# One-hot operands of the dense expert gates, built token by token instead of four tokens at a time

## The chip, the cores and the metric

The kernel runs on one core of a Trainium2 chip. The metric is the device time of one execution in microseconds (us). For the kernel before it is 4725.49 us, the median of 3 runs (4711.8 to 4730.83).

## What is computed

The reference is a two-layer trunk over 256 context and 512 latent tokens of width 1024. Each layer is a mixer followed by a PEER feed-forward: for every token, 8 heads select 16 of 16384 experts each, that is 128 pairs (e1, e2) with expert = 128·e1 + e2, and a softmax gate for each. The output is

```
act = gelu(sum_d pu[expert] * t) * gate
out = sum over the 128 chosen experts of act * pv[expert]
```

The change touches one step of this. For the tokens that are computed densely (all 16384 experts at once), the kernel needs a matrix G with G[e2, e1] = the sum of the gates of a token's chosen pairs (e1, e2), zero elsewhere, 128 x 128 numbers a token.

## The kernel before

Four of the latent token tiles (128 tokens each) of layer 0 and three of layer 1 are dense; the other tiles gather the rows of their experts from memory with an indirect DMA on POOL and add them up on DVE.

The function `peer` first routes (scores, top 16 by key half), then has a stage with two kinds of work in it. The first kind: `select` (lines 1034 to 1084) and `dense_gates` (lines 1086 to 1118) for each tile. The second: `up_part` (line 1228), which multiplies the tokens with one block of 128 experts of `pu` in 24 matmuls of f32r numbers (line 393), splits the weights into a high part on ACT (line 380) and a low part on DVE (line 383, tile `wlo`), and applies the gelu on ACT. 60 blocks of layer 0 and 48 of layer 1 are done there. Steps of the gather (lines 1127, 1132, 1141) are attached to them by `pace` and `gstep`. The next stage multiplies the gelu outputs with the gates, which it reads back from memory (tile `gt`, line 1290, all tiles of a block at once), so it starts when the last gates of the last tile have been written.

In `dense_gates` the 128 pairs of a token lie on the 128 partitions: e1, e2 and the gates are transposed (line 1095) and copied by ACT to SBUF (line 1096), the gates as a float16 high part and, on DVE (line 1097), a low part. Then, for every 4 tokens (`GW = 4`), DVE makes two tiles:

- `o`, two one-hot matrices (of e1 and of e2) for 4 tokens, by comparing a table of the numbers 0 to 127 (`iob`, line 248) with e1 and e2 (line 1105),
- `og`, the one-hot of e1 times the high and the low part of the gate (line 1107).

Both hold their numbers with the token as the innermost index, so that a token's 128 numbers lie 4 float16 numbers, or 8 bytes, apart. TensorE then makes G for each token in 2 matmuls of 128 columns (line 1113): the one-hot of e2 is the stationary operand, the two halves of `og` are the moving ones, and both add up in one piece of PSUM (`gps`). ACT copies it out in two pieces (line 1115) into `gbig`, and 64 tokens of it are written to memory with two DMAs of 2 MB (line 1118), issued from ACT's queue.

A dense tile has 32 such groups of 4 tokens: 128 groups in layer 0 and 96 in layer 1, 224 in all. `o` and `og` have 4 buffers each (`OB`), `gps` 3, `gbig` 3. The framework orders the instructions of each engine when the kernel is built, and each engine runs its queue in that order.

Of the kernel before, what the change touches and what calls it, by code (L numbers as in the profile page):

```python
# [8 lines left out]
F32 = mybir.dt.float32  # L9
F32R = mybir.dt.float32r  # L10
BF16 = mybir.dt.bfloat16
F16 = mybir.dt.float16
# [3 lines left out]
OP = mybir.AluOpType  # L16
# [16 lines left out]
GSC = 32768.0  # L33
GW = 4
# [34 lines left out]
OB = 4  # L69
# [126 lines left out]
class Net:  # L196
# [26 lines left out]
    def setup(self, st):  # L223
        tc, nc = self.tc, self.nc
        p = st.enter_context(tc.tile_pool(name="const", bufs=1))
        self.kt = p.tile(list(_CONST["consts"].shape), F32, name="kt")
        self.ct = p.tile([128, NCOLS], F32, name="ct")
        self.cc = p.tile([128, 8, 2], F32, name="cc")
        self.load(self.cc, self.I["cc"])
        self.load(self.kt, self.I["consts"])  # L230
        self.load(self.ct, self.I["cols"])
        self.eps = p.tile([128, 4], F32, name="eps")
        for j, v in enumerate((1e-6, 64e-5, 1e-5, 0.0)):
            nc.vector.memset(self.eps[:, j:j + 1], v)
        self.ones = p.tile([1, 2], F32, name="ones")
        nc.vector.memset(self.ones, 1.0)
        self.sc = p.tile([128, 8, 2], F32, name="sc")
        nc.scalar.activation(out=self.sc, in_=self.cc, func=AF.Silu)
        o = _COFF
        w = p.tile([128, 21], F32, name="shw")  # L240
        nc.vector.tensor_tensor(out=w, in0=self.cols("l0_shift_prev", 0, 21), in1=self.cols("l0_shift_next", 0, 21), op=OP.add)
        nc.vector.tensor_scalar(out=w, in0=w, scalar1=-1.0, scalar2=1.0, op0=OP.mult, op1=OP.add)
        self.shw = w
        ka = p.tile([128, 6], F32, name="ka1")
        nc.vector.tensor_scalar(out=ka, in0=self.cols("l0_k_a", 0, 6), scalar1=-1.0, scalar2=1.0, op0=OP.mult, op1=OP.add)
        self.ka1 = ka
        self.iob = p.tile([128, 128, GW], F16, name="iob")
        nc.vector.tensor_copy(self.iob, self.k("iota")[:, :, None].to_broadcast([128, 128, GW]))
        self.io16 = p.tile([128, 16, 16], BF16, name="io16")
        nc.vector.tensor_copy(self.io16, self.k("iota", 0, 16)[:, :, None].to_broadcast([128, 16, 16]))  # L250

        dp = st.enter_context(tc.tile_pool(name="modd", bufs=1, space=DR))
        self.odp = dp
        self.modd = [dp.tile([2, 6144], F32, name=f"modd{l}") for l in range(2)]
        self.modcol = [p.tile([128, 4, 8, 2], F32, name=f"modcol{l}") for l in range(2)]
# [830 lines left out]
    def dense_gates(self, e1, e2, gate, gd, sp, gp, pp, pt):  # L1086

        nc = self.nc
        V = nc.vector


        ee, gg = sp.tile([128, 2, 128], F16, name="gxe"), sp.tile([128, 2, 128], F16, name="gxg")
        for dst, x, sc in ((ee[:, 0], e1, 1.0), (ee[:, 1], e2, 1.0), (gg[:, 0], gate, GSC)):
            p = pt.tile([128, 128], F32, name="gtp")
            nc.tensor.transpose(p, x.rearrange("p a b -> p (a b)"), self.k("ident"))
            nc.scalar.mul(out=dst, in_=p, mul=sc)
        V.scalar_tensor_tensor(out=gg[:, 1], in0=p, scalar=GSC, in1=gg[:, 0], op0=OP.mult, op1=OP.subtract)
        W, H = GW, 64
        for h0 in range(0, 128, H):
            gh = [gp.tile([128, 64, H], F32, name="gbig") for _ in range(2)]  # L1100
            for t0 in range(h0, h0 + H, W):
                w = slice(t0, t0 + W)
                o = sp.tile([128, 2, 128, W], F16, name="o12", bufs=OB)
                og = sp.tile([128, 2, 128, W], F16, name="og", bufs=OB)
                V.tensor_tensor(out=o, in0=self.iob[:, None].to_broadcast([128, 2, 128, W]),
                                in1=ee[:, :, None, w].to_broadcast([128, 2, 128, W]), op=OP.is_equal)
                V.tensor_tensor(out=og, in0=o[:, 0:1].to_broadcast([128, 2, 128, W]),
                                in1=gg[:, :, None, w].to_broadcast([128, 2, 128, W]), op=OP.mult)
                for k0 in range(0, W, 4):
                    p = pp.tile([128, 4, 128], F32, name="gps")  # L1110
                    for j in range(4):
                        for i in range(2):
                            nc.tensor.matmul(p[:, j, :], o[:, 1, :, k0 + j], og[:, i, :, k0 + j], start=(i == 0), stop=(i == 1))  # L1113
                    for i, g in enumerate(gh):
                        nc.scalar.mul(out=g[:, :, t0 - h0 + k0:t0 - h0 + k0 + 4].rearrange("p e t -> p t e"), in_=p[:, :, i * 64:i * 64 + 64],  # L1115
                                      mul=1.0 / GSC)
            for i, g in enumerate(gh):
                nc.scalar.dma_start(gd[h0 // H, :, i * 64:i * 64 + 64, :], g)
# [501 lines left out]
```

## Time and profile before

| | before |
|---|---|
| median of 3 runs | 4725.49 us |
| the profiled execution | 4744.95 us |
| its span | 4743.2 us |
| mean granted TensorE clock | 0.944 |
| PE busy | 4296.7 us (91%) |
| DVE busy | 3613.7 us (76%) |
| ACT busy | 1705.7 us (36%) |
| POOL busy | 1687.5 us (36%) |

The span runs from the first to the last instruction of the profiled execution; some 2 us lie around it. Busy shares are means over stages with different limits. In the rows further down, L1113 is line 1113 of the kernel; PE is TensorE's matmul and PEld its weight load, which overlap; DVE is VectorE, ACT ScalarE, POOL GpSimd. A matmul's duration runs from its start to its modelled end, and consecutive matmuls overlap. "x128" counts instructions.

### The profile page before, as it was taken

To read this page: it belongs to the slowest core of one execution; us is meant where nothing else is said; L and a number is where in the kernel's file an instruction comes from. 1 tells how busy PE (TensorE), PEld (TensorE's weight loads), DVE (VectorE), ACT (ScalarE), POOL (GpSimd) and SP (SyncE) were. 2 spreads that over 40 slices of the span, in tenths; PEclk is the share of its full clock that TensorE was granted. 3 is DMA by queue.
4 is the path that set the end of the run, shared out by engine and by line. 5 is a ranking of instruction groups with operands and counts; after the bars stand their busy time and mean duration, and the time that the engine had idled before them with its cause. 6 is when DMAs were issued, how large, how long until landed. Compare 5 with 4: busy or idle time off the path is not lost.

```text
span 4743.2 us, 69779 instructions
## 1 busy us (share of the span) xinstructions
PE 4296.7 (91%) x26113; PEld 3547.1 (75%) x26113; DVE 3613.7 (76%) x6615; ACT 1705.7 (36%) x2825; POOL 1687.5 (36%) x1178
## 2 busy tenths in 40 slices
PE   7998899985869998999999999779999979999998
PEld 5775567874647887877777788666789968888887
DVE  2776566689889997877778787685499877788775
ACT  3443123332213555222222222346335543333333
POOL 2332112214644322444444443372321224444430
PEclk9998998987889998999999999889999979999999
DMA  4444773335778776888889888310235589999984
GB/s 165 100 107 105 267 258 116 113 121 167 229 245 284 251 261 244 309 309 302 299 311 308 302 302 281 117 35 25 86 111 189 211 318 331 329 336 338 333 289 152
DMA packets 487279, 1061.99 MB, mean 224 GB/s; under 512 B 95094, under 2 KB 265846, under 8 KB 477206
## 3 DMA queue, kind: packets, MB, share of 16 engines
q1 hardware_dynamic: 371740, 594.02, 38.2%
q0 software_dynamic: 110592, 402.70, 24.3%
q10 hardware_dynamic: 4608, 60.82, 3.1%
q8 instruction: 205, 3.36, 0.3%
q14 instruction: 134, 1.10, 0.1%
HBM read 927.83 MB, written 129.56 MB: 223 GB/s over the span
## 4 chain that ended last, share of the span: by engine, by line
PE 49%; DVE 15%; issue 14%; DMA 12%; POOL 8%; ACT 2%; SPq 0%; POOLq 0%; DVEq 0%; ACTq 0%
PE pS L393 14%; PE acc L1286 9%; POOL row L1127 7%; DMA row<-in_l_pv_dram,gi 6%; PE gps L1113 4%; PE sm L755 2%; DMA row<-in_l_pur_dram,gi 2%; PE pjl L393 2%; PE pq L393 2%; DVE row L1132 2%; PE aO L1567 1%; PE pjc L393 1%; PE sm L803 1%; PE acc L1315 1%; DVE rows L1141 1%
## 5 line engine op out<-in xcount | busy, mean ns | idle before, releaser
L1127 POOL DMA_INDIRECT row<-in_l_pv_dram,gi x384 | 541.6, 1411 | 874.4 <-DVE rows L1141 748.0
L393 PE MATMUL pS<-h2hi,wlo 128*128 128x512 f32 (+1 forms) x2048 | 753.9, 368 | 28.2 <-DVE wlo L383 28.2
L393 PE MATMUL pS<-h2hi,whi 128*128 128x512 f32 (+1 forms) x2048 | 755.1, 369 | 19.9 <-ACT a L1232 14.8
L393 PE MATMUL pS<-h2lo,whi 128*128 128x512 f32 (+1 forms) x2048 | 752.8, 368 | 0.0
L1127 POOL DMA_INDIRECT row<-in_l_pur_dram,gi x384 | 482.7, 1257 | 696.7 <-DVE ga L1132 519.9
L380 ACT CAST whi<-wraw 128x1024 fp32r<-128x1024 f32 x327 | 344.2, 1054 | 825.7 <-PE pS L393 644.3
L1132 DVE CUSTOM_DVE_ANT_0 row<-row,rows 128x1024 f32<-128x1024 f32 x384 | 486.7, 1272 | 196.6 <-DMA row<-in_l_pur_dram,gi 195.2
L1141 DVE SCALAR_TENSOR_TENSOR rows<-row,ga,rows 128x1024 f32<-128x1024 f32 x381 | 496.7, 1304 | 157.0 <-DMA row<-in_l_pv_dram,gi 154.8
L1286 PE MATMUL acc<-vhi,ahi 128*128 128x512 f32 x1536 | 470.1, 392 | 12.9 <-ACT ahi L380 12.8
L1286 PE MATMUL acc<-vlo,ahi 128*128 128x512 f32 x1536 | 479.3, 392 | 1.8 <-DVE vlo L383 1.7
L1286 PE MATMUL acc<-vhi,alo 128*128 128x512 f32 x1536 | 470.3, 391 | 0.4 <-DVE alo L383 0.4
L393 PEld LDWEIGHTS pS<-h2hi,wlo 128*128 128x128 f32 x2048 | 390.6, 191 | 72.9 <-DVE wlo L383 32.0
L393 PEld LDWEIGHTS pS<-h2hi,whi 128*128 128x128 f32 x2048 | 391.2, 191 | 66.8 <-ACT a L1232 15.7
L393 PEld LDWEIGHTS pS<-h2lo,whi 128*128 128x128 f32 x2048 | 391.0, 191 | 43.5
L383 DVE TENSOR_TENSOR wlo<-wraw,whi 128x1024 fp32r<-128x1024 f32 x266 | 342.0, 1286 | 58.6 <-ACT whi L380 58.0
L380 ACT CAST vhi<-vraw 128x1024 fp32r<-128x1024 f32 x256 | 265.2, 1051 | 232.8 <-DMA vraw<-in_l_pv_dram 113.1
L383 DVE TENSOR_TENSOR vlo<-vraw,vhi 128x1024 fp32r<-128x1024 f32 x256 | 309.7, 1220 | 43.8 <-ACT vhi L380 43.5
L1286 PEld LDWEIGHTS acc<-vhi,ahi 128*128 128x128 f32 x1536 | 287.7, 188 | 69.3 <-ACT ahi L380 15.1
L1286 PEld LDWEIGHTS acc<-vlo,ahi 128*128 128x128 f32 x1536 | 289.4, 189 | 64.8 <-DVE vlo L383 3.3
L1286 PEld LDWEIGHTS acc<-vhi,alo 128*128 128x128 f32 x1536 | 288.6, 188 | 62.9 <-DVE alo L383 2.2
L380 ACT CAST ahi<-a32f 128x384 fp32r<-128x384 f32 (+1 forms) x148 | 83.5, 564 | 613.1 <-DVE a32f L1302 312.6
L1115 ACT ACTIVATE gbig<-gps 128x256 f32<-128x256 f32 x448 | 235.5, 660 | 165.5 <-PE gps L1113 141.2
(459 smaller groups left out, 8306.8 us busy)
## 6 DMA issues: line engine op xcount, KB each, us to landing
wraw<-in_l_pu_dram SPq DMA_DIRECT2D x256, 512.0 KB
vraw<-in_l_pv_dram SPq DMA_DIRECT2D x256, 512.0 KB
gd<-gbig ACTq DMA_DIRECT2D x28, 2048.0 KB
mw<-in_l_mod_w_dram SPq DMA_DIRECT2D x48, 1024.0 KB
gt<-gd SPq DMA_DIRECT2D x64, 512.0 KB
wraw<-in_l_pq_dram SPq DMA_DIRECT2D x48, 512.0 KB
gt<-gd SPq DMA_DIRECT2D x64, 384.0 KB
ab<-arb SPq DMA_DIRECT2D x24, 768.0 KB
```

The source lines that it names most:

```text
L380: e.copy(out=hi, in_=src)
L383: return (e_lo or nc.vector).tensor_tensor(out=lo, in0=src, in1=hi.bitcast(F32), op=OP.subtract)
L393: nc.tensor.matmul(ps, a[:, k, :], b[:, k, t0:t0 + n], start=s, stop=e)
L755: self.nc.tensor.matmul(ps[q, i, :], fa(par, i), fb(par, i), start=True, stop=True)
L803: nc.tensor.matmul(ps[par][:, i, :], bk[PH[par], j], ar[PH[par], j], start=True, stop=True)
L1113: nc.tensor.matmul(p[:, j, :], o[:, 1, :, k0 + j], og[:, i, :, k0 + j], start=(i == 0), stop=(i == 1))
L1115: nc.scalar.mul(out=g[:, :, t0 - h0 + k0:t0 - h0 + k0 + 4].rearrange("p e t -> p t e"), in_=p[:, :, i * 64:i * 64 + 64], mul=1.0 / GSC)
L1127: nc.gpsimd.indirect_dma_start(out=r, out_offset=None, in_=self.I[f"l{l}_{src}"], in_offset=bass.IndirectOffsetOnAxis(ap=idx[:, s:s + 1], ...
L1132: V.tensor_tensor_reduce(out=r, in0=r, in1=acc, scale=1.0, scalar=0.0, op0=OP.mult, op1=OP.add, accum_out=act[:, s:s + 1])
L1141: V.scalar_tensor_tensor(out=acc, in0=r, scalar=act[:, s:s + 1], in1=acc, op0=OP.mult, op1=OP.add)
L1286: nc.tensor.matmul(acc[t][h2], x[:, q], y[:, h2 * 512:(h2 + 1) * 512], start=s, stop=z)
L1315: nc.tensor.matmul(p, x[:, 384:512], y[:, c], start=s, stop=z)
```

## The change

Each token's numbers now lie next to each other, and gate and one-hot are made in one operation. The table `iob` has one copy of 0 to 127 instead of four. The tile `o` holds the one-hot of e2 only. For each token DVE runs three TENSOR_SCALAR instructions over 128 float16 numbers: one compares the table with the token's e2 (one number for each partition, read from a column of `ee`), two compare it with e1 and multiply by the high or the low part of the gate (two numbers for each partition, from columns of `ee` and `gg`). Since those columns are read as scalars, `ee` and `gg` are float32 now; the gate's high part is first rounded to float16 (`g16`) and copied back, one more ACT instruction a tile. Matmuls, PSUM, the copies out and the DMAs stay as they are.

```diff
-        self.iob = p.tile([128, 128, GW], F16, name="iob")
-        nc.vector.tensor_copy(self.iob, self.k("iota")[:, :, None].to_broadcast([128, 128, GW]))
+        self.iob = p.tile([128, 128], F16, name="iob")
+        nc.vector.tensor_copy(self.iob, self.k("iota"))
...
-        ee, gg = sp.tile([128, 2, 128], F16, name="gxe"), sp.tile([128, 2, 128], F16, name="gxg")
-        for dst, x, sc in ((ee[:, 0], e1, 1.0), (ee[:, 1], e2, 1.0), (gg[:, 0], gate, GSC)):
+        ee, gg = sp.tile([128, 2, 128], F32, name="gxe"), sp.tile([128, 2, 128], F32, name="gxg")
+        for dst, x in ((ee[:, 0], e1), (ee[:, 1], e2), (None, gate)):
             p = pt.tile([128, 128], F32, name="gtp")
             nc.tensor.transpose(p, x.rearrange("p a b -> p (a b)"), self.k("ident"))
-            nc.scalar.mul(out=dst, in_=p, mul=sc)
+            if dst is not None:
+                nc.scalar.copy(out=dst, in_=p)
+        g16 = sp.tile([128, 128], F16, name="gx16")
+        nc.scalar.mul(out=g16, in_=p, mul=GSC)
+        nc.scalar.copy(out=gg[:, 0], in_=g16)
         V.scalar_tensor_tensor(out=gg[:, 1], in0=p, scalar=GSC, in1=gg[:, 0], op0=OP.mult, op1=OP.subtract)
...
-                w = slice(t0, t0 + W)
-                o = sp.tile([128, 2, 128, W], F16, name="o12", bufs=OB)
-                og = sp.tile([128, 2, 128, W], F16, name="og", bufs=OB)
-                V.tensor_tensor(out=o, in0=self.iob[:, None].to_broadcast([128, 2, 128, W]),
-                                in1=ee[:, :, None, w].to_broadcast([128, 2, 128, W]), op=OP.is_equal)
-                V.tensor_tensor(out=og, in0=o[:, 0:1].to_broadcast([128, 2, 128, W]),
-                                in1=gg[:, :, None, w].to_broadcast([128, 2, 128, W]), op=OP.mult)
+                o = sp.tile([128, W, 128], F16, name="o12", bufs=OB)
+                og = sp.tile([128, 2, W, 128], F16, name="og", bufs=OB)
+                for j in range(W):
+                    t = slice(t0 + j, t0 + j + 1)
+                    V.tensor_scalar(out=o[:, j], in0=self.iob, scalar1=ee[:, 1, t], scalar2=None, op0=OP.is_equal)
+                    for i in range(2):
+                        V.tensor_scalar(out=og[:, i, j], in0=self.iob, scalar1=ee[:, 0, t], scalar2=gg[:, i, t],
+                                        op0=OP.is_equal, op1=OP.mult)
...
-                            nc.tensor.matmul(p[:, j, :], o[:, 1, :, k0 + j], og[:, i, :, k0 + j], start=(i == 0), stop=(i == 1))
+                            nc.tensor.matmul(p[:, j, :], o[:, k0 + j], og[:, i, k0 + j], start=(i == 0), stop=(i == 1))
```

## Rows read from the trace of the kernel before

**Rows 1.** Busy us by stretch: stretch, length, PE, PEld, DVE, ACT, POOL, clock, DMA.

```profile
1480.00:1810.00 330.00, 330.00 (x1813) 276.88 (x1812) 311.15 (x542) 171.49 (x289) 111.58 (x66) 1.00 0.73 258
1810.00:1860.00 50.00, 37.67 (x283) 32.11 (x281) 40.60 (x67) 36.42 (x73) 0.00 (x0) 0.71 0.52 212
3560.00:3780.00 220.00, 218.16 (x1421) 210.83 (x1419) 196.33 (x373) 130.41 (x222) 46.60 (x15) 1.00 0.54 194
3780.00:3840.00 60.00, 38.47 (x262) 34.62 (x262) 52.19 (x84) 30.34 (x59) 14.54 (x12) 0.70 0.72 260
```

**Rows 2.** The chain that ended last, 1380 to 1960 us: start, us, what.

```profile
1474.39 14.97 PE pS L393 x66
1489.36 2.85 PE gps L1113 x24
...
1817.16 8.19 DMA gd<-gbig
...
1861.73 7.21 PE pS L393 x23
```

**Rows 3.** DVE's groups, 1480 to 1860 us: busy, mean ns, idle before.

```profile
L1105 DVE TENSOR_TENSOR o<-iob,gxe 128x1024 f16<-128x1024 f16 x128 | 89.0, 713 | 20.5 <-PE gps L1113 19.5 <-ACT gxe L1096 0.9
L1107 DVE TENSOR_TENSOR og<-o,gxg 128x1024 f16<-128x1024 f16 x128 | 84.7, 684 | 0.1
L383 DVE TENSOR_TENSOR wlo<-wraw,whi 128x1024 fp32r<-128x1024 f32 x46 | 63.1, 1372 | 4.3 <-ACT whi L380 4.0
L1141 DVE SCALAR_TENSOR_TENSOR rows<-row,ga,rows 128x1024 f32<-128x1024 f32 x33 | 50.6, 1533 | 0.0
...
L1066 DVE TENSOR_SCALAR tb<-taf 128x128 f32<-128x128 bf16 x3 | 0.7, 221 | 0.0
```

**Rows 4.** DVE's timeline behind the last up part of layer 0: start, us, what.

```profile
1829.71 0.69 DVE L1107 TENSOR_TENSOR og<-o,gxg 128x1024 f16<-128x1024 f16 x1
1830.32 0.69 DVE L1105 TENSOR_TENSOR o<-iob,gxe 128x1024 f16<-128x1024 f16 x1
```

**Rows 5.** Other DVE operations, whole span: by line (min/median/max ns) or by group.

```profile
L1081 DVE TENSOR_TENSOR tex<-teq,txf x8: 1205/1222/2310, 1096.3 to 1157.5; 128x1024 f32<-128x1024 bf16 x8
...
L1319 DVE TENSOR_TENSOR acc<-acc,acc 128x512 f32<-128x512 f32 x126 | 86.3, 685 | 9.2 <-PE acc L1315 9.2
...
L315 DVE TENSOR_SCALAR nx<-nx,ns 128x1024 f32<-128x1024 f32 x6 | 4.5, 754 | 0.2
L600 DVE TENSOR_SCALAR kds<-ag,ct,ka 128x768 f32<-128x768 f32 x6 | 4.0, 674 | 0.0
...
L336 DVE TENSOR_SCALAR nh<-pt,modcol x32: 396/410/413, 1143.6 to 3398.5; 128x128 f32<-128x128 f32 x32
```

**Rows 6.** DVE's timeline around two TENSOR_SCALARs in a row.

```profile
1143.62 0.72 DVE L336 TENSOR_SCALAR nh<-pt,modcol 128x128 f32<-128x128 f32 x2
1144.26 0.68 DVE L990 TENSOR_TENSOR ox<-ox,om 128x512 f32<-128x512 f32 x1
```

**Rows 7.** TensorE, whole span: line 1113 (min/median/max ns) and groups of line 393.

```profile
L1113 PEld LDWEIGHTS <-o x1792: 111/117/147, 1489.2 to 3843.6; 128*128 128x128 f16 x200
L1113 PE MATMUL gps<-og,o x1792: 273/297/330, 1489.2 to 3843.7; 128*128 128x128 f16 x200
...
L393 PE MATMUL pS<-h2lo,whi 128*128 128x512 f32 x1024 | 404.3, 395 | 0.0
L393 PE MATMUL pS<-h2lo,whi 128*128 128x384 f32 x1024 | 348.5, 340 | 0.0
...
L393 PEld LDWEIGHTS pS<-h2lo,whi 128*128 128x128 f32 x2048 | 391.0, 191 | 43.5
```

**Rows 8.** ACT's copy of the gates ahead of a tile's groups, by line.

```profile
L1096 ACT ACTIVATE gxg<-gtp x7: 270/278/320, 1474.5 to 3761.8; 128x128 f16<-128x128 f32 x7
```

**Rows 9.** The full stretches of rows 1, line 1113 alone: PE, PEld, clock, DMA.

```profile
1480.00:1810.00 330.00, 97.73 (x750) 81.03 (x751) 1.00 0.73 258
...
3560.00:3780.00 220.00, 69.94 (x536) 57.86 (x536) 1.00 0.54 194
```

## The prediction

> **What bounds the kernel now.** I began with the busy time by slice, where the two stages in which gates are made stand out by a full TensorE, and cut them into stretches [rows 1]. In layer 0 (1480 to 1810 us) PE is busy for all of 330 us, at full clock; but DVE is busy for 311.15 of them as well. Then comes a tail of 50 us in which only gates are left: the clock is down to 0.71 and no engine is full. Layer 1 has the same shape: 220 us with PE at 218.16 and DVE at 196.33, and a tail of 60 us. So two engines are nearly full, and what the change takes from the one and gives to the other decides.
>
> The chain of waits for that time [rows 2] goes through PE: up-part matmuls (66 in 14.97 us, 227 ns apart) in turn with gate matmuls (24 in 2.85 us, 119 ns apart), in the tail through gates and the 2 MB writes of them (8.19 us), and the first work of the next stage starts at 1861.73, behind the last gates. That stage's end is thus the end of the gates, wherever they are held up.
>
> In DVE's groups of the stage [rows 3] the two instructions of the gates take 89.0 and 84.7 us for 128 groups. They share the queue with the low parts of the weights (63.1 us), on which the up-part matmuls wait, with the steps of the gather (50.6 us at line 1141), by which POOL gets its row buffers back, and with the selection of the next tile. DVE runs its queue in order, so whatever is added to a group delays all of these.
>
> **The change part by part: DVE.** Removed are 2 TENSOR_TENSORs for 4 tokens. In a row they start 0.60 us apart, with a duration of 0.685 [rows 4]: 85 ns of each lie under its neighbour. A group costs 2 x 600 = 1200 ns.
>
> Added are 12 TENSOR_SCALARs of 128 numbers: 4 that read one column as their scalar and 8 that read two. The trace has no such instruction in float16, so I build its price from the nearest rows.
> - Rate. A TENSOR_TENSOR of f32 takes 685 ns for 512 numbers and 1222 for 1024, so 1.05 ns a number [rows 5]; the float16 one does 1024 in 685 [rows 4], twice as fast.
> - Fixed part. If TENSOR_SCALAR of f32 takes half of 1.05 ns a number, what is left is 221 - 67 = 154 ns with no column (line 1066) [rows 3], 754 - 537 = 217 with one (line 315), 674 - 403 = 271 with two (line 600) [rows 5]. Each column costs about 60 ns.
> - Does the column's part hide under the instruction before it? Two instructions of line 336, 410 ns each alone and with two columns [rows 5], take 0.72 us together, and the next starts 0.64 after the first [rows 6]: 320 each, 90 hidden, no more than with TENSOR_TENSOR. It doesn't hide.
> - Numbers. If float16 doubles the rate of TENSOR_SCALAR as it does that of TENSOR_TENSOR, 128 numbers take 33 ns; if not, 67. I take 33, because the doubling is what the nearest float16 row shows, and keep 67 for the range.
>
> So one column costs 33 + 217 - 87 = 163 ns, two cost 33 + 271 - 87 = 217, and a group 4 x 163 + 8 x 217 = 2388 ns, twice the 1200 of before. At 67 ns it is 2796. The lower bound is a column that costs nothing: 12 x (33 + 154 - 87) = 1200, no difference at all. [...]
>
> On DVE that adds 1188 ns x 128 = 152 us to layer 0 and x 96 = 114 us to layer 1, 266 in all. DVE's idle time in these stretches is 380 - 351.75 = 28 us and 280 - 248.52 = 31 us [rows 1]; part of it is the wait for buffers in the tails, which slower gates hide. I count half of it as used up: 266 - 30 = **236 us**, with 206 and 266 as the bounds.
>
> **TensorE.** All 1792 gate matmuls get contiguous operands. The weight load is short already, 117 ns against 191 for f32 [rows 7], so I expect nothing there. The matmul is not: f32r takes 395 ns for 512 columns and 340 for 384, 55 for 128 columns, which would make 230 for 128; float16 at a step of 8 bytes takes 297 [rows 7]. That 67 ns more, and the 119 ns from one matmul to the next [rows 2] where the f32r pace of 227 for 512 (213 of columns and 14) would give 67, say that the step costs some 52 ns a matmul. The gain lies between 0 and 52 x 1792 = 93 us of PE time. I count it at nothing for the span: with DVE full, PE waits for splits and one-hots, and a faster matmul makes that wait longer. What hides it is DVE's added 266 us; without that cover the gain is a rival below.
>
> **The rest.** One more ACT copy a tile at 278 ns [rows 8], with the low part of the gate waiting for it: at most 7 x 0.3 = 2 us if nothing covered it, but ACT is half idle [rows 1] and DVE has other tiles' work; I count 1. The smaller table is made once, at the start, and I count nothing for it. No DMA is added or moved. POOL's gathers wait longer for row buffers within the stage; their number there is fixed, and their end is not what the next stage waits for. ACT's copies out of PSUM come later, not more often.
>
> **Sum.** 4744.95 + 236 + 1 = 4982 us for the profiled execution. That execution stood 19.5 us above the median of the runs; against the median it is 4725.49 + 237 = **4962 us**, and the forecast's own range 4930 to 4995.
>
> **The rivals.**
> 1. *The columns are free, and TensorE was the bound (faster).* If the fetch of the columns runs under the instruction before, a group stays at 1200 ns. Then DVE is unchanged and PE's 52 ns count: in the full stretches the 750 gate matmuls of layer 0 [rows 9] give 39 us, cut off by DVE's idle 330 - 311 = 19, and the 536 of layer 1 give 28, cut off at 220 - 196 = 24 [rows 1]. That is -43 us, 4682. The point from which it decides is a group of some 1300 ns; line 336 speaks against it, since its two columns did cost in a row [rows 6]. Chance 0.13. [...]
> 2. *Columns are free and the layout does nothing for PE (no change).* The 119 ns would then come from something other than the step. Time 4725, chance 0.04. [...]
> 3. *No doubling.* 2796 - 1200 = 1596 ns x 224 = 358, less 30: 5053. Line 1066 with a 16-bit input and an f32 output doesn't tell. Chance 0.15.
> 4. *TensorE's clock.* With PE waiting, the clock may fall as in the tails (0.71 and 0.70 [rows 1]). [...] Chance 0.07.
> 5. *Columns half hidden.* A group of about 1800 ns: 134 less 30, 4830. Chance 0.05.
>
> **How the numbers follow.** The forecast has 0.56. A measurement of this kernel can tell about 0.5% (24 us) from no change. Faster by more is rival 1, 0.13; the same is rival 2, 0.04; the rest is slower, 0.83. The range from 4825 to 5085 holds the forecast and rivals 3 to 5, 0.83 together, with the upper bound of rival 3; likeliest alone, 4930 to 4995.
>
> **What would show it.** In the changed profile 2688 TENSOR_SCALARs stand in place of the 448 TENSOR_TENSORs, at about 250 ns (896) and 304 ns (1792); 284 and 338 if float16 doesn't double. Twelve in a row take 2.4 us. DVE is busy for over 95% of two stages that end some 140 and 95 us later, PE's idle time ahead of lines 393 and 1113 names DVE, and the clock there lies under 1.00. The gate matmuls take about 235 ns, some 67 apart where they run in a row. The forecast is wrong if twelve take under 1.5 us, or if the order of DVE's queue, which is made anew when the kernel is built, puts splits and gates so that PE finishes its up parts much later than the gates.

## The result, and the profile after

The changed kernel takes 5052.85 us (median of 4 runs, 5043.1 to 5054.38), the kernel before 4728.16 in the runs beside it: a ratio of 1.0681 with a 95% interval of 1.0659 to 1.0702, or some 325 us more by the medians. The forecast was 4962, its range 4825 to 5085.

The page of the kernel after, its busy times and three of its strips (40 slices of 126 us):

```profile
span 5041.3 us, 72050 instructions
PE 4440.3 (88%) x26113; PEld 3500.4 (69%) x26113; DVE 3886.5 (77%) x8855; ACT 1711.7 (34%) x2832; POOL 1649.6 (33%) x1178
PE   7997999967678679999999999779978779999998
DVE  2776576798999996677778888674699977787675
PEclk9997999978878658999999999899988579999999
```

DVE's busy time has grown from 3613.7 to 3886.5 us, by 273. In both stages with the gates (slices 12 to 15 and 31 to 32) its strip now reads 9, and there the strips of PE and of its clock have fallen.

DVE's and TensorE's groups of the gates (busy, mean ns of one, idle before). Lines 1111 and 1113 are the new one-hots and gates, 1119 the matmul that was 1113:

```profile
L1113 DVE TENSOR_SCALAR og<-iob,gxe,gxg 128x128 f16<-128x128 f16 x1792 | 524.2, 345 | 0.0
L1111 DVE TENSOR_SCALAR o<-iob,gxe 128x128 f16<-128x128 f16 x896 | 243.6, 279 | 2.0 <-ACT gxe L1097 2.0
...
L1119 PE MATMUL gps<-og,o 128*128 128x128 f16 x1792 | 380.7, 255 | 176.3 <-DVE og L1113 113.4 <-ACT gbig L1121 1.1 <-issue 0.2
```

DVE's timeline in layer 0's stage, two tokens in a row (start us, us, what):

```profile
1702.29 0.56 DVE L1113 TENSOR_SCALAR og<-iob,gxe,gxg 128x128 f16<-128x128 f16 x2
1702.74 0.28 DVE L1111 TENSOR_SCALAR o<-iob,gxe 128x128 f16<-128x128 f16 x1
1702.90 0.56 DVE L1113 TENSOR_SCALAR og<-iob,gxe,gxg 128x128 f16<-128x128 f16 x2
```

A token takes 1702.90 - 1702.29 = 0.61 us, a group of four some 2.43 us; before it was 1.20 [rows 4]. An instruction with one column starts 0.16 us before the next (1702.74 to 1702.90), one with two columns some 0.22 (half of 1702.29 to 1702.74). TensorE's idle time ahead of the gate matmuls names DVE for 113.4 of 176.3 us, as it had to.

Then the stages. Busy us by stretch (stretch, length, PE, PEld, DVE, ACT, POOL, clock, DMA) of the kernel after; layer 0 from its first gate to its last and from there to the next stage, then layer 1 the same way:

```profile
1473.00:1916.00 443.00, 332.86 (x1542) 179.40 (x1541) 441.76 (x1821) 176.77 (x322) 59.17 (x36) 0.67 0.36 135
1916.00:2061.00 145.00, 138.75 (x596) 113.77 (x597) 74.32 (x64) 42.20 (x54) 37.59 (x29) 0.97 0.87 305
...
3732.00:4075.00 343.00, 251.37 (x1291) 155.17 (x1289) 339.67 (x1377) 139.58 (x252) 35.27 (x24) 0.67 0.34 124
4075.00:4173.00 98.00, 83.77 (x442) 82.81 (x442) 56.63 (x75) 30.06 (x41) 34.26 (x25) 0.90 0.95 353
```

The same four stretches of the kernel before:

```profile
1489.00:1862.00 373.00, 360.46 (x2065) 303.08 (x2064) 342.74 (x586) 207.74 (x363) 108.96 (x63) 0.96 0.70 250
1862.00:1883.00 21.00, 18.19 (x71) 14.19 (x72) 6.67 (x8) 6.83 (x10) 1.14 (x1) 0.92 0.93 344
...
3570.00:3844.00 274.00, 248.79 (x1647) 237.39 (x1647) 241.31 (x437) 155.95 (x276) 63.55 (x29) 0.93 0.59 212
3844.00:3874.00 30.00, 18.89 (x98) 18.57 (x97) 16.48 (x22) 8.68 (x12) 8.80 (x7) 0.78 1.01 396
```

This is not the picture that the prediction drew. While gates are made, DVE is full (1.2 us idle out of 443) and PE waits, at a clock of 0.67. After the last gate comes a second part, 145 and 98 us long, in which PE works off up parts at a clock of 0.97 and 0.90 while DVE is about half idle. Before the change the next stage began 21 and 30 us behind the last gate. A split is the low part of one block's weights, made on DVE (line 383); the 24 matmuls of an up part go with it. The splits (line 383 alone) in the same stretches, first of the kernel before:

```profile
1489.00:1862.00 373.00, 61.90 (x45) 0.96 0.70 250
1862.00:1883.00 21.00, 3.15 (x4) 0.92 0.93 344
```

and of the kernel after:

```profile
1473.00:1916.00 443.00, 24.62 (x21) 0.67 0.36 135
1916.00:2061.00 145.00, 37.99 (x32) 0.97 0.87 305
```

So 45 splits stood among the gates of layer 0 in these stretches, and now 21 do; counted from DVE's first gate instruction to its last, as in the table below, it is 46 and 20. Most of the rest come behind the gates, and the 24 matmuls of each up part with them. The first matmul of the next stage starts, in the kernel before and in the kernel after (the first line of each pair is layer 0, the second layer 1):

```profile
1883.29 1.07 PE L1286 MATMUL acc<-vhi,ahi 128*128 128x512 f32 x4
...
3873.96 1.22 PE L1286 MATMUL acc<-vhi,ahi 128*128 128x512 f32 x2 [11.11 <-ACT ahi L380]
```

```profile
2061.08 0.61 PE L1292 MATMUL acc<-vhi,ahi 128*128 128x512 f32 x2
...
4173.52 0.63 PE L1292 MATMUL acc<-vhi,ahi 128*128 128x512 f32 x2
```

Layer 0's stage ends 2061.1 - 1883.3 = 178 us later (some 140 forecast), layer 1's 4173.5 - 3874.0 = 299.6, another 122 (95 forecast). From there to the end the two kernels take the same time, 4743.2 - 3874.0 = 869 and 5041.3 - 4173.5 = 868 us.

Theory from these rows: DVE's doubled price is the cause, as predicted, and the order in which the builder (the framework, which orders each engine's instructions when the kernel is built) lays DVE's queue adds to it, since up parts that find no place between gates run behind them. Rivals: the number of instructions costs and not what they read; something else in the change costs; order has no effect.

### The profile page after: what moved, and what is told of

It reads as the page before. It is cut to its first block, busy times and chain, and to the rows that moved or that the text cites. A ratio compares the mean times of both kernels' runs of the same rounds, so it can differ in the third digit from the quotient of the medians.

```text
span 5041.3 us, 72050 instructions
## 1 busy us (share of the span) xinstructions
PE 4440.3 (88%) x26113; PEld 3500.4 (69%) x26113; DVE 3886.5 (77%) x8855; ACT 1711.7 (34%) x2832; POOL 1649.6 (33%) x1178
## 4 chain that ended last, share of the span: by engine, by line
PE 42%; DVE 24%; issue 14%; DMA 10%; POOL 7%; ACT 2%; SPq 0%; POOLq 0%; DVEq 0%; ACTq 0%
PE acc L1292 11%; PE pS L393 10%; DVE og L1113 6%; POOL row L1133 6%; DMA row<-in_l_pv_dram,gi 5%; DMA row<-in_l_pur_dram,gi 2%; DVE o L1111 2%; PE sm L755 2%; DVE row L1138 2%; PE pjl L393 2%; PE pq L393 2%; PE acc L1321 2%; DVE te L1082 1%; PE aO L1573 1%; PE pjc L393 1%
## 5 line engine op out<-in xcount | busy, mean ns | idle before, releaser
L393 PE MATMUL pS<-h2hi,wlo 128*128 128x512 f32 (+1 forms) x2048 | 764.1, 374 | 37.0 <-DVE wlo L383 37.0
L393 PE MATMUL pS<-h2hi,whi 128*128 128x512 f32 (+1 forms) x2048 | 766.6, 374 | 33.8 <-ACT a L1238 29.6
L393 PE MATMUL pS<-h2lo,whi 128*128 128x512 f32 (+1 forms) x2048 | 763.1, 373 | 0.0
L1119 PE MATMUL gps<-og,o 128*128 128x128 f16 x1792 | 380.7, 255 | 176.3 <-DVE og L1113 113.4
L1113 DVE TENSOR_SCALAR og<-iob,gxe,gxg 128x128 f16<-128x128 f16 x1792 | 524.2, 345 | 0.0
L1119 PEld LDWEIGHTS <-o 128*128 128x128 f16 x1792 | 157.8, 104 | 401.0 <-DVE o L1111 164.9
L383 DVE TENSOR_TENSOR wlo<-wraw,whi 128x1024 fp32r<-128x1024 f32 x266 | 329.1, 1243 | 129.1 <-ACT whi L380 123.7
```

The source lines that it names most:

```text
L383: return (e_lo or nc.vector).tensor_tensor(out=lo, in0=src, in1=hi.bitcast(F32), op=OP.subtract)
L393: nc.tensor.matmul(ps, a[:, k, :], b[:, k, t0:t0 + n], start=s, stop=e)
L1113: V.tensor_scalar(out=og[:, i, j], in0=self.iob, scalar1=ee[:, 0, t], scalar2=gg[:, i, t], op0=OP.is_equal, op1=OP.mult)
L1119: nc.tensor.matmul(p[:, j, :], o[:, k0 + j], og[:, i, k0 + j], start=(i == 0), stop=(i == 1))
```

## The experiments

All runs in one table. "Splits" counts the splits between the first and the last gate instruction of layer 0 and of layer 1 on DVE, from each run's trace (some of the expectations, made from the queue as built, differ by one, those of gatecol2 by three); "layout" is the step at which TensorE reads a token's numbers.

| run | group on DVE, us | splits | layout | time, us | ratio to before (95%) |
|---|---|---|---|---|---|
| before | 1.20 | 46 / 39 | 8 bytes | 4728 | 1 |
| after | 2.43 | 20 / 20 | contiguous | 5052.85 | 1.0681 (1.0659 to 1.0702) |
| imm | 1.22 | 46 / 39, in lumps | contiguous | 4776.95 | 1.0098 (1.0078 to 1.0118) |
| imm2_ob3 | 1.22 | 45 / 39, even | contiguous | 4700.53 | 0.9934 (0.9908 to 0.9960) |
| gatecol2 | 1.95 | 48 / 42 | contiguous | 4851.45 | 1.0265 (1.0244 to 1.0286) |
| after_ob2 | 2.43 | 46 / 39 | contiguous | 4973.35 | 1.0521 (1.0504 to 1.0539) |
| after_ob3 | 2.43 | 36 / 21 | contiguous | 5012.36 | 1.0593 (1.0572 to 1.0614) |
| stride | 2.43 | 21 / 19 | 8 bytes | 5068.39 | 1.0711 (1.0680 to 1.0742) |
| double | 2.49 | 46 / 39 | 8 bytes | 4999.63 | 1.0578 (1.0544 to 1.0613) |
| double_contig | 2.49 | 46 / 39 | contiguous | 4983.33 | 1.0524 (1.0500 to 1.0548) |
| bcast | 2.27 | 46 / 39 | contiguous | 4877.60 | 1.0305 (1.0274 to 1.0337) |
| contig | 1.20 | 46 / 39 | contiguous | 4706.15 | 0.9946 (0.9926 to 0.9966) |
| pair | 1.20 | 46 / 39 | 4 bytes | 4703.04 | 0.9940 (0.9917 to 0.9964) |
| pair_pool | 1.20 and waits | 36 / 30 | 4 bytes | 4713.18 | 0.9970 (0.9952 to 0.9988) |

### What the columns cost: imm, imm2_ob3, gatecol2

imm takes the columns away and leaves number, size and layout of the instructions:

```diff
-  V.tensor_scalar(out=o[:, j], in0=self.iob, scalar1=ee[:, 1, t], ...)
+  V.tensor_scalar(out=o[:, j], in0=self.iob, scalar1=3.0, ...)
-  V.tensor_scalar(out=og[:, i, j], in0=self.iob, scalar1=ee[:, 0, t], scalar2=gg[:, i, t], ...)
+  V.tensor_scalar(out=og[:, i, j], in0=self.iob, scalar1=5.0, scalar2=0.5, ...)
```

> The changed kernel, but the twelve TENSOR_SCALARs of a group take constants (3.0; 5.0 and 0.5) where they read columns, so the one-hots and gates are those of one fixed pair of keys; number, size and layout of the instructions stay. Theory (the columns are the price): without them an instruction costs 33 + 154 - 87 = 100 ns in a row, a group 1.2 us instead of the 2.43 of the changed kernel; DVE is back at its price of before, PE keeps its shorter gate matmuls, and the kernel takes 4680 to 4740 us. Rival (it is the number of instructions, 12 in place of 2, whatever they read): a group stays at 2.4 us and the kernel at 5040 to 5065. Half way (columns are part of it): a group of 1.8 us, some 4850.

DVE's timeline of imm:

```profile
1633.18 0.28 DVE L1113 TENSOR_SCALAR og<-iob 128x128 f16<-128x128 f16 x2
1633.39 0.18 DVE L1111 TENSOR_SCALAR o<-iob 128x128 f16<-128x128 f16 x1
1633.49 0.28 DVE L1113 TENSOR_SCALAR og<-iob 128x128 f16<-128x128 f16 x2
```

A token takes 1633.49 - 1633.18 = 0.31 us, a group 1.22 us: half of the changed kernel's, with the same twelve instructions. The columns are the price, and the number of instructions is not. But the time missed its range: 4777, not 4680 to 4740. Three stretches of layer 0's stage (columns as above):

```profile
1650.00:1675.00 25.00, 13.68 (x104) 9.52 (x104) 25.00 (x133) 15.05 (x27) 9.24 (x4) 0.81 0.27 105
1675.00:1700.00 25.00, 13.97 (x70) 11.10 (x69) 25.00 (x123) 5.59 (x12) 7.21 (x3) 0.64 0.43 171
1700.00:1725.00 25.00, 23.28 (x182) 16.73 (x180) 24.39 (x167) 21.75 (x38) 8.31 (x4) 1.00 0.63 230
```

PE is nearly half idle in two of the three, with DVE full. In imm the queue has runs of 14 and 27 groups without a split, and since its one-hots no longer depend on the selection, DVE also makes some ahead of it (the first at 1390 us, where it was 1471). imm2_ob3 was built to have neither: it reads a tile that depends on the selection, and three buffers spread the splits.

```diff
-OB = 4
+OB = 3
-  V.tensor_scalar(out=o[:, j], in0=self.iob, scalar1=3.0, ...)
+  V.tensor_scalar(out=o[:, j], in0=g16, scalar1=3.0, ...)
-  V.tensor_scalar(out=og[:, i, j], in0=self.iob, scalar1=5.0, scalar2=0.5, ...)
+  V.tensor_scalar(out=og[:, i, j], in0=g16, scalar1=5.0, scalar2=0.5, ...)
```

> The changed kernel with constants in place of columns once more, but reading a tile that depends on the selection (the gates of the tile of tokens, so that nothing can be made ahead of it) and with three buffers: the builder now spreads 45 and 39 splits evenly over the gates, with last runs of 10 gates without a split. The one-hots and gates are meaningless. Theory (in the run with constants before, runs of up to 27 gates without a split kept PE waiting, which cost what its shorter matmuls gave): a group is still 1.2 us and the kernel takes 4680 to 4735 us. Rival (twelve small instructions cost more than their own time, in handshakes with PE): 4765 to 4790, as in the run before.

4700.53 us, and the same stretches:

```profile
1650.00:1675.00 25.00, 23.30 (x137) 17.67 (x136) 25.00 (x93) 14.62 (x25) 11.82 (x5) 1.00 0.79 295
1675.00:1700.00 25.00, 22.97 (x143) 18.35 (x142) 25.00 (x102) 11.95 (x24) 8.24 (x5) 1.00 0.50 161
1700.00:1725.00 25.00, 25.00 (x164) 20.48 (x163) 22.99 (x137) 15.76 (x28) 8.02 (x6) 1.00 0.98 388
```

At the same price of a group PE is nearly full, and the kernel is 76 us faster than imm. The pair differs in dependence, buffers and order together, so it doesn't prove the order alone; the next runs do more for that.

gatecol2 takes only the gate's column away (12 columns a group in place of 20), with two buffers:

```diff
-  ... scalar1=ee[:, 0, t], scalar2=gg[:, i, t], ...
+  ... scalar1=ee[:, 0, t], scalar2=0.5, ...
-OB = 4
+OB = 2
```

> The changed kernel with a constant (0.5) in place of the gate's column, so the gates are all the same and every TENSOR_SCALAR reads one column; two buffers, which put 46 and 39 splits among the gates. Theory (every column costs the same 61 ns, and DVE's time goes through to the kernel's nearly one to one): a group has 12 columns in place of 20, 1.22 + 12 x 0.061 = 1.95 us; between 4700 us at 1.22 us a group and 4973 at 2.43, both with splits spread among the gates, that gives 4700 + 273 x 0.73 / 1.21 = 4865 us, 4835 to 4890. Rival 1 (the first column of an instruction carries all of the price): 2.3 us a group or more, 4930 to 4970. Rival 2 (the second column does): 1.5 us or less, 4730 to 4780.

DVE's timeline of gatecol2:

```profile
1850.44 0.25 DVE L1111 TENSOR_SCALAR o<-iob,gxe 128x128 f16<-128x128 f16 x1
1850.60 0.41 DVE L1113 TENSOR_SCALAR og<-iob,gxe 128x128 f16<-128x128 f16 x2
1850.93 0.25 DVE L1111 TENSOR_SCALAR o<-iob,gxe 128x128 f16<-128x128 f16 x1
```

A token takes 0.49 us, a group 1.95, as computed ahead, and the kernel 4851 us, inside the range. Per token: 0.305 us with no column, 0.49 with three, 0.61 with five, so (0.49 - 0.305) / 3 = 62 ns for each of the first three and (0.61 - 0.49) / 2 = 60 ns for each of the others. First and second column of an instruction cost the same, and both rivals fall.

### What the order costs: after_ob2, after_ob3

```diff
-OB = 4
+OB = 2      # after_ob3: 3
```

These are the changed kernel with fewer buffers for the one-hots, and the builder lays DVE's queue differently.

> The changed kernel with two buffers instead of four for o12 and og, which makes the builder put 46 and 39 splits of up parts among the gates of the two layers, as before the change, in place of 20 and 20. Nothing else changes; the work of every engine is the same. Theory (the order of DVE's queue cost the rest: up parts that found no place between gates run after them on PE while DVE idles): DVE's price of a group stays at 2.4 us, the gates end later, the stages end earlier, by 40 to 75 us in layer 0 and 20 to 45 in layer 1, and the kernel takes 4940 to 5000 us. Rival 1 (DVE's added time alone makes the difference, in whatever order): 5035 to 5070. Rival 2 (with two buffers DVE waits for PE between groups, and that costs more than the order gives): above 5070.

> The changed kernel with three buffers: the builder puts 36 splits among the gates of layer 0 and 21 among those of layer 1, where four buffers gave 20 and 20 and two gave 46 and 39. Theory (what counts is how many splits stand among the gates): layer 0's next stage starts most of the 48 us earlier that two buffers gave, layer 1's hardly changes, and the time is 5005 to 5035 us, between 5053 and 4973. Rival (it was something else in having two buffers): 4965 to 4985 or 5045 to 5065.

After_ob2: line 383 alone in layer 0's gates, then all work in the four stretches (first gate to last, and from there to the next stage):

```profile
1477.00:1990.00 513.00, 56.63 (x46) 0.79 0.51 185
...
1477.00:1990.00 513.00, 438.64 (x2093) 271.15 (x2092) 505.27 (x1875) 212.12 (x367) 105.00 (x64) 0.79 0.51 185
1990.00:2013.00 23.00, 18.78 (x72) 14.66 (x71) 7.95 (x9) 8.08 (x11) 2.75 (x2) 0.89 0.93 332
...
3697.00:4080.00 383.00, 296.63 (x1670) 205.04 (x1669) 376.33 (x1413) 161.92 (x282) 57.62 (x37) 0.76 0.47 164
4080.00:4104.00 24.00, 18.46 (x95) 18.14 (x94) 12.89 (x20) 8.46 (x12) 7.53 (x6) 0.86 0.98 381
```

46 splits stand among the gates again. Layer 0's gates end 74 us later than in the changed kernel, and the stage 48 us earlier, for the second part has shrunk from 145 us to 23. The next stages start at:

```profile
2013.18 1.52 PE L1292 MATMUL acc<-vhi,ahi 128*128 128x512 f32 x6
...
4104.49 2.07 PE L1292 MATMUL acc<-vhi,ahi 128*128 128x512 f32 x4 [6.03 <-ACT vhi L380]
```

That is 130 us later than before in layer 0 and 230.5 - 129.9 = 101 more in layer 1. The kernel takes 4973 us, 80 less than the changed one, with every instruction the same. With three buffers, and splits in number between the two in layer 0 only, it takes 5012, between the two. The forecast of that run had layer 0 alone gaining; its stages start at 2032.60 and 4140.17 us, 28 and another 5 us earlier. With 20, 36 and 46 splits among layer 0's gates the times fall in that order. What two buffers cost in waits for PE is small: DVE's idle time ahead of line 1111 that names line 1119 is 3.9 us in the whole run.

### Is it DVE's time, or something else? double, double_contig, stride

double is the kernel before with two more TENSOR_TENSORs a group into a tile that nobody reads:

```diff
   V.tensor_tensor(out=og, ...)
+  for _ in range(2):
+      V.tensor_tensor(out=self.dum, in0=self.iob..., in1=ee..., op=OP.is_equal)
```

> The kernel before, with two further float16 TENSOR_TENSORs of 1024 numbers in each group of four tokens, written to a tile that nobody reads: DVE pays 4 x 600 = 2400 ns for a group, as after the change, but there are no columns, no new layout, and TensorE's gate matmuls stay at 119 ns apart. The builder puts 45 and 39 splits among the gates, as before. Theory (the price on DVE is what the change costs, and the order of the queue adds to it): 1.2 us x 224 = 269 us less what of DVE's idle it fills, 4935 to 5000 us. Rival 1 (DVE's price alone, order without effect): 5035 to 5070, like the changed kernel. Rival 2 (something else of the change costs, DVE's time is covered): 4730 to 4830.

4999.63 us, at the upper end of the theory's range. The profile's group of the addition, and fifteen of them behind the last gate of layer 0:

```profile
L1110 DVE TENSOR_TENSOR dum<-iob,gxe 128x1024 f16<-128x1024 f16 x448 | 317.4, 709 | 5.9
...
1979.33 10.83 DVE L1110 TENSOR_TENSOR dum<-iob,gxe 128x1024 f16<-128x1024 f16 x15
```

Between other instructions an addition takes 0.60 us from start to start, but behind another addition (10.83 - 0.68) / 14 = 0.725. 172 of the 448 stand so, which makes a group 2.40 + 172 x 0.12 / 224 = 2.49 us. 41 and 43 of the additions run behind the last gates of the two layers, so they are not all part of the gates' pace. Without a column and without a new layout DVE's busy time grows from 3613.7 to 3887.8 us, by 274, and the time by 270 against the kernel before beside it: DVE's time alone makes a loss of the size that the changed kernel has with as many splits among its gates (after_ob2, 244 against the kernel before beside it).

stride is the changed kernel with TensorE reading at a step of 8 bytes (which gives it numbers of several tokens, so G itself is not made):

```diff
-  nc.tensor.matmul(p[:, j, :], o[:, k0 + j], og[:, i, k0 + j], ...)
+  nc.tensor.matmul(p[:, j, :], os_[:, :, k0 + j], ogs[i][:, :, k0 + j], ...)   # step of 4 numbers
```

> The changed kernel, with TensorE reading the same tiles at a step of 4 numbers (the wrong tokens' numbers, in the layout of before). DVE's work is unchanged. Theory (in the changed kernel the new layout gives TensorE time that nobody waits for, since DVE sets the pace of the gates): gate matmuls go back to 297 ns, 119 apart, and the time stays at 5035 to 5075 us. Rival (TensorE's gain is at work in the changed kernel, DVE's price was even larger than the difference of the times shows): 62 ns x 1792 = 111 us more, up to 5160.

```profile
L1121 PE MATMUL gps<-og,o 128*128 128x128 f16 x1792 | 271.4, 295 | 288.6 <-DVE og L1113 287.4 <-ACT gbig L1123 1.1
```

The matmul is back at 295 ns, and the time, 5068, cannot be told from the changed kernel's: the intervals overlap. (A token's matmuls also read numbers of the whole group here, so they start later in the group than in the changed kernel; that cost nothing that can be seen either.) double_contig asks the same of double, in the same order instruction by instruction:

```diff
-  nc.tensor.matmul(p[:, j, :], o[:, 1, :, k0 + j], og[:, i, :, k0 + j], ...)
+  nc.tensor.matmul(p[:, j, :], oc[:, 512 + 128 * j:640 + 128 * j], ogc[:, 512 * i + 128 * j:512 * i + 128 * j + 128], ...)
```

> The kernel with two further TENSOR_TENSORs a group, with TensorE reading 128 numbers next to each other (those of several tokens); the order of DVE's queue is the same as without, instruction by instruction, and a group costs DVE 2.4 us in both. It asks what the shorter gate matmuls are worth while DVE pays double. Theory 1 (they count where TensorE is full, with up parts between the gates: 51 groups of layer 0 and 44 of layer 1 before the long last runs of gates, 95 x 8 x 62 ns = 47 us, and nothing in the last runs, where DVE sets the pace): 4940 to 4970 us in place of 5000. Theory 2 (DVE bounds all of it, they count nothing): 4985 to 5015. Theory 3 (they explain why the run with operands repeated in place, 2.26 us a group, took 4878): 4890 to 4925.

4983, only 16 us less than double, and the intervals still touch. My estimate of 47 us was too high. With DVE at 2.5 us a group TensorE's shorter matmuls are worth little.

### The layout without columns: contig, pair, bcast, pair_pool

contig leaves DVE as before and lets TensorE read 128 numbers in a row, those of several tokens, so G itself is not made:

```diff
+  oc, ogc = (x.rearrange("p a k w -> p (a k w)") for x in (o, og))
-  nc.tensor.matmul(p[:, j, :], o[:, 1, :, k0 + j], og[:, i, :, k0 + j], ...)
+  nc.tensor.matmul(p[:, j, :], oc[:, 512 + 128 * j:640 + 128 * j], ogc[:, 512 * i + 128 * j:512 * i + 128 * j + 128], ...)
```

> The kernel before, DVE untouched, but TensorE reads 128 numbers next to each other out of the tiles (which are then those of several tokens). It gives the second half of the change alone. Theory (PE's side of the change is a gain that only an unchanged DVE lets through): gate matmuls some 57 ns apart and not 119, 62 ns x 1792 = 111 us of PE's time, of which DVE's idle time in the two stages (19 and 24 us where PE is full) lets at most 43 through: 4685 to 4715 us. Rival (DVE sets the pace already before the change): 4720 to 4740.

pair computes the same as the kernel before, two tokens to a pair of neighbouring numbers:

```diff
-  o = sp.tile([128, 2, 128, W], F16, ...)        # og alike
+  o = sp.tile([128, 2, 2, 128, 2], F16, ...)
-  nc.tensor.matmul(p[:, j, :], o[:, 1, :, k0 + j], og[:, i, :, k0 + j], ...)
+  nc.tensor.matmul(p[:, j, :], o[:, 1, j // 2, :, j % 2], og[:, i, j // 2, :, j % 2], ...)
```

> The kernel before, with the four tokens of a group laid out as two pairs: the numbers of two tokens alternate, so TensorE reads a token at a step of 4 bytes where it was 8, and DVE still makes a group with two TENSOR_TENSORs of 1024 numbers. Theory (with DVE's price unchanged TensorE's shorter gate matmuls count, as far as DVE follows): DVE stays at 0.60 us an instruction, gate matmuls start some 60 to 90 ns apart where it was 119, and the time is 4685 to 4720 us. Rival 1 (TensorE's pace decides nothing, or a step of 4 bytes is no better than 8): 4720 to 4740. Rival 2 (runs of two numbers lose the doubled rate of float16 on DVE): 1.1 to 1.2 us an instruction, 4940 to 5010.

Gate matmuls in a row on TensorE, first of the kernel before, then of contig, then of pair:

```profile
1489.20 3.01 PE L1113 MATMUL gps<-og,o 128*128 128x128 f16 x24
```

```profile
1494.69 1.51 PE L1114 MATMUL gps<-og,o 128*128 128x128 f16 x24
```

```profile
1701.94 1.55 PE L1115 MATMUL gps<-og,o 128*128 128x128 f16 x24
```

In the kernel before they start (3.01 - 0.30) / 23 = 118 ns apart. In contig and pair it is (1.51 - 0.22) / 23 = 56 and (1.55 - 0.22) / 23 = 58 ns: a step of 4 bytes is as good as none. contig gives 4706 us, pair 4703. That is 25 and 28 us under the kernel before, inside the ranges, and below the cut-off of 43. pair is faster than both kernels of this case, than the kernel before by 0.6%; its interval, 0.9917 to 0.9964, excludes 1.

bcast keeps the change's layout and goes back to two TENSOR_TENSORs, which read a token's key 128 times in place:

```diff
+  S4 = [128, 2, W, 128]
+  V.tensor_tensor(out=o, in0=self.iob[:, None, None].to_broadcast(S4),
+                  in1=ee[:, :, w, None].to_broadcast(S4), op=OP.is_equal)
```

> The layout of the change (token by token, contiguous) with the two TENSOR_TENSORs of before: the key and the gate of a token are read 128 times in place (a step of 0 in the innermost dimension), and no TENSOR_SCALAR is left. It asks whether the layout or the columns carry the price. If an operand that is repeated in the innermost dimension keeps float16's doubled rate: 0.60 us an instruction, group 1.2 us, contiguous matmuls, 4685 to 4715 us. If it loses the doubling: 1.1 to 1.2 us an instruction, group 2.2 to 2.4 us, and with 45 and 38 splits among the gates 4940 to 5000 us. I hold the second for likelier, at 0.7.

```profile
1896.93 3.49 DVE L1106 TENSOR_TENSOR o<-iob,gxe 128x1024 f16<-128x1024 f16 x3
```

Three take 3.49 us, some 1.13 each (start to start) where it was 0.60: the doubled rate is lost, and the likelier case came. Yet the time, 4878, is under the range, and 106 us under double_contig (111 by the two spans, 4988.6 and 4877.2). The price of a group accounts for (2.49 - 2.27) x 224 = some 50 us. Another 41 is work that lies elsewhere. The steps of the gather on DVE in layer 1's stage, first of double_contig, then of bcast (stretch, length, DVE, clock, DMA):

```profile
3706.00:4118.00 412.00, 41.12 (x67) 0.76 0.53 187
```

```profile
3666.00:4010.00 344.00, 0.00 (x0) 0.79 0.44 166
```

bcast makes these steps behind the stage, where DVE has idle time for them: from there to the end the two take 4988.6 - 4117.7 = 871 and 4877.2 - 4009.7 = 867 us. The last 20 us stay open. So the same 41 us of work on DVE cost their time in one stage and nothing that shows in the other, by the place that the queue gave them.

pair_pool moves every fourth split of pair from DVE to POOL:

```diff
-  *u, i = self.wtile(up, self.I[f"l{l}_pu"][b], e_lo=V, q=nc.sync)
+  *u, i = self.wtile(up, self.I[f"l{l}_pu"][b], e_lo=G if b % 4 == 3 else V, q=nc.sync)
```

> The kernel with the pairs, with every fourth low part of the up parts' weights made by POOL, not by DVE, which is full in the stages of the gates (319 of 330 us). Theory (DVE bounds these stages with the pairs): 10 and 8 splits of 1.2 us leave DVE in the two stages, and 4675 to 4698 us come out in place of 4703. Rival (POOL's splits stand behind gathers that wait for DVE, and TensorE waits for them): 4710 to 4780.

4713, no gain on pair (the intervals overlap), and not by the rival's way either: TensorE waits for POOL's splits for 1.8 us in layer 1's stage and not at all in layer 0's. DVE's groups of pair_pool, and one instruction of POOL and of DVE at the same time:

```profile
L1107 DVE TENSOR_TENSOR o<-iob,gxe 128x1024 f16<-128x1024 f16 x224 | 174.4, 799 | 9.0 <-PE gps L1115 9.0
L1109 DVE TENSOR_TENSOR og<-o,gxg 128x1024 f16<-128x1024 f16 x224 | 167.9, 771 | 0.1
...
1703.95 3.35 POOL L383 TENSOR_TENSOR wlo<-wraw,whi 128x1024 fp32r<-128x1024 f32 x1 [5.91 <-ACT whi L380]
1705.16 2.70 DVE L1107 TENSOR_TENSOR o<-iob,gxe 128x1024 f16<-128x1024 f16 x1
```

In pair the means were 704 and 703 ns. 64 splits (83.4 us) have left DVE, and its busy time over the whole run still rose from 3605.9 to 3644.6 us, because what is left on it takes longer, these two groups by 38.6 us. The means mislead: the medians stay where they were, 680 and 679 ns after 682. What grows is the number that take over 1 us, from 6 to 26 of 448. Each of the 26 runs beside a TENSOR_TENSOR of POOL and ends 0.55 us behind it, as in the two rows (1707.86 and 1707.30): it is as if DVE's instruction stood until POOL's had ended. What these 26 take beyond the median is 47 us, 10 for the 6 of pair, which is nearly all of the growth of the two groups.

## Why the prediction was right, and where its size was off

1. **The price of a group: right.** 2388 ns were forecast, 2.43 us measured. Columns cost 60 to 62 ns each (60 forecast) and do not hide under the instruction before; float16's doubled rate holds for 128 numbers, since an instruction without columns starts 1.22 / 12 = 102 ns after the last (100 forecast, 134 without doubling). Rival 1's condition (columns free), rival 3's (no doubling) and rival 5's (half hidden) are each excluded by one timeline. (That the rate is doubled rests on the fixed part read at line 1066, 154 ns; line 1554 of the kernel before, a TENSOR_SCALAR on a single f32 number without a column, takes 154 ns too, the median of 48.) One of the signs named ahead pointed the other way: the durations, 279 and 345 ns in the mean, lie nearer to the 284 and 338 named for no doubling than to 250 and 304. They vary between runs of the same instructions (261 and 317 in after_ob2), while the starts stay 163 and 223 ns apart, as forecast; more of each lies under its neighbour, and the distance of the starts is what DVE pays.
2. **DVE's added time: right, and most of it goes through.** With as many splits among the gates as before, the changed kernel takes 245 us more (after_ob2), where 237 were forecast; its stages end 130 and 101 us later, where "some 140 and 95" stood. Between imm2_ob3 and after_ob2 a group grows by 1.21 us, 271 us for 224 groups, and the time by 273; to gatecol2 by 0.73 us, 164, and the time by 151. It is no law: from pair to bcast a group grows by 1.07 us, 240, and the time by 175, with steps of the gather moved out of the stage. The prediction held that their number in a stage is fixed; in layer 1's it is 21 before, 34 in the changed kernel (24 of them behind the last gate) and none in bcast.
3. **"I count half of it as used up": the step that failed.** It took DVE's idle time to fall by 30 us, as if the old order stayed. Over the four stretches DVE was idle for 30 + 14 + 33 + 14 = 91 us before; in the changed kernel it is 1 + 71 + 3 + 41 = 117. There is next to none while gates are made, and more than ever behind them, where PE works off the up parts alone. So idle time rose by 26 instead of falling by 30. Over the whole span it rose from 4743.2 - 3613.7 = 1129.5 to 5041.3 - 3886.5 = 1154.8 us, by 25; with DVE's 273 us more of busy time that is the 298 between the two spans. In after_ob2 idle time in the four stretches is 8 + 15 + 7 + 11 = 41, a fall of 50. That the order makes the difference is shown by after_ob2 and after_ob3, not by this sum. The prediction had named the queue's new order as what would make it wrong, and put no price on it.
4. **TensorE's gain counted at nothing: right while DVE pays double** (stride, double_contig: 16 us at most, not told from none). Without that cover it is 25 to 31 us (contig, pair, imm2_ob3), less than rival 1's 43, although the matmuls come to lie 57 ns apart, closer than the 67 that were named.
5. **The clock.** It fell, to 0.67 in both gate stretches, as rival 4 said. No run takes it apart from the rest; but where it is lowest PE waits for DVE (busy for 332.86 of 443 us and 251.37 of 343, with DVE at 441.76 and 339.67), and the up parts behind the gates run at 0.97 and 0.90, so I see no room for a loss that the clock makes by itself; that is argued, not shown.

That the time, 5053, equals rival 3's number is chance: its mechanism is absent. By the medians the loss is 245 us for DVE's price with the old number of splits (after_ob2) and 80 for the order. That the range held the time is luck in part: it was drawn up to 5085 for rivals 3 to 5, and the order, which had no price, used that room; the narrower forecast, 4930 to 4995, missed.

## What to carry to other kernels

A per-partition column as the scalar of a DVE instruction was not free here, at 60 to 62 ns each: count the columns, at the price that a pair of rows of the same kernel shows, before trading a few large instructions for many small ones. When a change makes one engine's step longer, the builder may lay the queue anew, so look at how many of the other work's instructions stand between the long ones, before and after: here that was a quarter of the loss. And a layout that serves TensorE need not be contiguous; runs of two float16 numbers of two tokens (pair) kept DVE's large instructions, at 0.60 us each, and let TensorE start a gate matmul every 58 ns, where contiguous numbers gave 56.

## What I had not expected

- A step of 4 bytes is as good for float16 gate matmuls as contiguous numbers (58 and 56 ns apart, in pair and contig); a step of 8 bytes costs 118.
- The number of buffers of a small tile set the order of another loop's work: two are 80 us faster than four in the changed kernel.
- With 12 splits on POOL in layer 0's stage, a few of DVE's float16 TENSOR_TENSORs lasted until an instruction of POOL had ended, up to 3.3 us, and the others took as long as ever. Each of the 26 long ones ended 0.55 us behind POOL's. In the changed kernel 24 of the 2688 TENSOR_SCALARs take over 1 us, each ending 0.05 us behind a TENSOR_TENSOR of POOL; beyond the medians that is 40 us, 11 for the 7 of the kernel before, and the prediction had no term for it.
